# Hybrid decoder step: low weight parts on GpSimd for the last tiles, later splits, longer yields at four places

## Chip, cores and metric

One core of one Trainium2 chip. The metric is device microseconds (us) of one execution, as the median of repeated runs. Engines: PE (TensorE; PEld is its weight load), DVE (VectorE), ACT (ScalarE), POOL (GpSimd), SP (SyncE, which issues most DMAs).

## What is computed

Two layers of a hybrid decoder trunk over 520 tokens (512 of a prompt and 8 samples of one token each), width 2048, float32. Each layer is, cut to what matters:

```python
mod = silu(c) @ w_ada + b_ada                     # shift, scale, gate
h = rms_norm(x, norm_g) * (1 + scale) + shift
proj = h @ w_in                                   # 53 column tiles of 128
att = attend(rope(q), rope(k), v, sinks)          # window 128, 16 query heads, 4 key heads
mixed = cur + (prev - cur) * mu_shift             # r, kr, vr, decay and rate inputs
ys, S_T = wkv_recurrence(r, decay, k_eff, v, kk, a, S0)
y_rw = group_norm(ys) * ln_w + ln_b + bonus
out = concat([att * silu(g_att), y_rw * silu(g_rw)]) @ w_out
x = x + gate * out
```

A final RMSNorm follows; keys, values, recurrent states and shifts are outputs as well.

## The kernel before

The two large products hold weights as the stationary operand, 128x128, and move 260 tokens at a time. To keep float32 precision each weight is split into a high part (rounded) and a low part (the rest), the activations too, and a product is the sum of three: high by high, high by low, low by high. The loop over this is `quarter` (line 372): a weight tile of 2048x128 is done in four quarters of 128x512 weights, and a quarter is 4 x 3 x 2 = 24 matmuls (line 380). A layer has 53 such tiles for `w_in`, in the order of `ORDER`, then 16 for `w_out`. The tiles of a layer come as: the low-rank tile L; then eight groups of three (P: r, kr, v of two recurrent heads) with gate tiles (R, and the first three A) between; then keys and values (K, V, K, V); then eight query tiles (Q); one gate tile A; and the last four A.

**Weights.** `load_w` (line 343) has SP load a quarter's 256 KB into one of four `raw` buffers. `head_w` has ACT cast it to the high part (line 355, four `hi` buffers). `split_w` (line 357) has DVE subtract to get the low part (line 365, three `lo` buffers), and then issues the load that takes the freed `raw` buffer. `quarter` calls `split_w(n + 3)` after its last matmul, so high cast, low part and load stand in their engines' queues right behind the quarter, and the low part has to wait until PE is through with the quarter whose buffer it takes.

**Side work.** Everything else (norms, modulation, attention, the recurrence) is written as Python generators. Each main matmul ticks a counter (`Side.tick`), and at most one generator that is due runs up to its next `yield`, whose value (mostly from the list `W`) is the distance in main matmuls to its next piece. So the order of the work in every engine's queue is fixed by these distances; the engines then run it in order, waiting on each other's results. Some places drain side work, that is emit the rest with no main matmul between: at the gate tile A4 until all eight attentions and all eight chains are done (`RELOAD`), and at the layer's end until the samples are.

The pieces that the change touches:

- `ada` (line 273) computes the modulation. For its last third, run beside the first tiles of a layer, it loads `GA` steps ahead; each step is 40 main matmuls, and the products (line 299) run for two steps together.
- `chain` (line 535), one per pair of recurrent heads: 64x64 triangular inverses are made from two 32x32 inverses each. The matrices go through DRAM (line 647 out by SP, line 662 in by POOL), POOL runs 31 steps of two instructions (lines 670 and 672) on the 32x32 inverses, stores them (line 714), clears `xT` (lines 717, 718) and loads them back (line 721). Then two products join the halves: line 733, a copy on DVE (line 736), `yield W[30]` (4), line 741, a copy (line 745), `yield W[31]` (3). The sequence steps (lines 763 to 787) follow.
- `attend` (line 912), one per query tile: rope, high part of the query on ACT, low parts on DVE (line 931, twice, `yield W[79]` (6) behind each), then scores (lines 949, 950), softmax, transposes (982), products (993).
- `attend_samples` (line 1015), once all query tiles are roped: eight rounds, one per sample: copy of the new key (line 1034), `yield W[61]` (4), scores (1041), softmax, transpose (1060), product (1067). A join of all samples (line 1075) and the gating follow.

In the out projection the first two tiles run quarter by quarter together, and only then does DVE add their residual (line 1190); the third tile takes the first one's accumulator. At the start of layer 0 tiles are done in parts of one quarter, which DVE adds up (line 404).

Of the kernel before, what the change touches and what calls it, by code (L numbers as in the profile page):

```python
# [12 lines left out]
ALU = mybir.AluOpType  # L13
# [6 lines left out]
KT = 16  # L20
# [19 lines left out]
NT = 53  # L40
# [59 lines left out]
ORDER = _order()  # L100
# [4 lines left out]
LOG = 30  # L105
INV = 95
DEPTH = 3
RMS = 29
HQ = 4
LEAD0 = 3  # L110
GA = 1
ADA0 = 70
GROUP = 4
HT = 3
# [17 lines left out]
W = [0, 0, 10, 3, 32, 10, 12, 24, 15, 19, 4, 16, 4, 3, 30, 4, 3, 5, 4, 4, 4, 5, 13, 9, 8, 6, 24, 24, 152, 13, 7, 3, 9, 9, 14, 10, 4, 29, 30, 13, 12, 12, 4, 20, 12, 36, 9, 40, 5, 12, 1, 10, 6, 6, 19, 12, 12, 4, 4, 77, 24, 4, 23, 12, 11, 2, 10, 6, 10, 6, 26, 3, 13, 9, 3, 9, 11, 13, 11, 6]  # L132
# [39 lines left out]
def body(ctx, tc, xt, ct, consts, pars, wada, win, wout, lora, sst, swkv, ck, cv, cvn, fing,  # L172
         o_y, o_kp, o_vp, o_sp, o_sh, o_ks, o_vs, o_vn, o_ss):
    nc = tc.nc
    ve, se, ge, pe, sy = nc.vector, nc.scalar, nc.gpsimd, nc.tensor, nc.sync
# [156 lines left out]
    wseq = []  # L332
# [7 lines left out]
    held = [(NT + KT + i, q) for q in range(HQ) for i in range(2)]  # L340
    raws, his, splits = {}, {}, {}

    def load_w(n):
        if n < len(wseq):
            i, q = wseq[n][:2]
            raws[n] = wp.tile([128, 4, 128], F32, tag="raw", name="raw", bufs=RAWS)
            sy.dma_start(out=raws[n], in_=wsrc[i][:, 4 * q:4 * q + 4, :])
# [9 lines left out]
    def split_w(n):  # L357
        if n < len(wseq):
            hi = his.pop(n)
            head_w(n + 1)  # L360
            if wseq[n] in held:
                lo = t2([128, 512], "wlo", F32R).rearrange("p (k c) -> p k c", k=4)
            else:
                lo = wp.tile([128, 4, 128], F32R, tag="lo", name="lo", bufs=DEPTH)
            ve.tensor_tensor(out=lo, in0=raws.pop(n), in1=hi, op=ALU.subtract)  # L365
            splits[wseq[n]] = (n, hi, lo)
            load_w(n + RAWS)

# [3 lines left out]
    def quarter(ps, key, hh, hl, k0=0, k1=KT, halves=(0, 1)):  # L372


        n, hi, lo = splits[key]
        for k in range(4 * key[1], 4 * key[1] + 4):
            for j, (a, b) in enumerate(((hi, hh[k]), (hi, hl[k]), (lo, hh[k]))):
                for h in halves:
                    stop = k == k1 - 1 and j == 2
                    pe.matmul(ps[:, h, 0:NH], a[:, k % 4], b[:, h * NH:(h + 1) * NH],  # L380
                              start=(k == k0 and j == 0), stop=stop)
                    if not stop:
                        side.tick()
        if key not in held or halves[-1]:
            del splits[key]
        if key not in held or not halves[0]:
            split_w(n + DEPTH)

    def gemm(i, hh, hl, name):

# [108 lines left out]
    def layer(l, hh, hl, xprev, xnext, start, prepare, after):  # L499
# [35 lines left out]
        def chain(p, lw, r, kr, v):  # L535
# [95 lines left out]
            for g in range(2):  # L631
# [8 lines left out]
                for h in range(2):  # L640
                    for a, o in ((atk[g], 64), (atq[g], 0)):
                        ve.tensor_tensor(out=a[:, :, h], in0=pss[h][:, :, o:o + 64],
                                         in1=wmask[:, o:o + 64].unsqueeze(1).to_broadcast([128, 4, 64]),
# [90 lines left out]
            for i in range(2):  # L734
                o = (96, 64)[i]
                ve.tensor_copy(x1[96:128, i], pa[o:o + 32, 0:8])
            yield W[30]
            for e in range(8):
                for i in range(2):
                    o = (64, 96)[i]  # L740
# [2 lines left out]
            for i in range(2):  # L743
                o = (64, 96)[i]
                ve.tensor_copy(flat(xT[i])[64:96, :, 32:64], pa[o:o + 32, 8:16])
            yield W[31]
            y = t2([128, N], "y")
            for c in range(8):
                if c == 6:
# [162 lines left out]
        def attend(P, m, ps):  # L912
# [16 lines left out]
            for u in range(2):  # L929
                us = slice(64 * u, 64 * u + 64)  # L930
                ve.tensor_tensor(out=qq[u][64 - 64 * u:128 - 64 * u], in0=q[us, 0:T], in1=qq[u][us],
                                 op=ALU.subtract)
                yield W[79]
            ya = t2([128, T], "ya")
            col = 8 * P + 2 * m
            kk, kl = kT[P]
            for n0 in range(0, 4, 2):
# [3 lines left out]
                for u in range(2):  # L941
# [3 lines left out]
                    for i in range(2):  # L945
                        n = n0 + i
# [68 lines left out]
        def attend_samples():  # L1015
# [15 lines left out]
            for b in range(B):  # L1031
                load(b + 1)
                for P in range(2):
                    ve.tensor_copy(kc[b][:, P, 128:129], kS[P][:, b:b + 1])
                yield W[61]
                sy.dma_start(out=o_ks[l, :, :, b, :], in_=kc[b][:, :, 1:129])
                ps = ps1("ssc")
                for kv in range(4):
# [455 lines left out]
```

## Time and profile before

| what | value |
|---|---|
| median of 3 runs | 2344.32 us (2335.37 to 2345.83) |
| profiled execution | 2349.78 us, span 2348.0 us |
| mean granted PE clock | 0.975 |
| PE busy | 2223.8 us (95%) |
| PEld busy | 2104.7 us (90%) |
| DVE busy | 1482.8 us (63%) |
| ACT busy | 1057.9 us (45%) |
| POOL busy | 794.7 us (34%) |
| layer 0: w_in tiles, w_out tiles | 45 to 1000.7 us, 1000.8 to 1221.9 us |
| layer 1: w_in tiles, w_out tiles | 1222 to 2141.2 us, 2141.3 to 2330.9 us |

The profile is one execution: the span runs from the first to the last instruction, and the execution is longer by what lies around it. Busy times are shares of the span. A granted clock of 1.00 is 2.4 GHz and 0.50 is 1.2 GHz. In a row of a timeline the bracket is the idle time of the engine before it, and what ended it.

### The profile page before, as it was taken

What the parts mean: (1) busy time and instruction counts of PE and PEld (TensorE: products, weight loads), DVE (VectorE), ACT (ScalarE), POOL (GpSimd) and SP (SyncE); (2) the same over time, 40 slices, a digit from 0 to 9 for tenths busy, and PEclk for the clock granted to TensorE, in tenths of its full rate; (3) what the DMA queues carried; (4) which work ended last, traced back from release to release, by engine and by line L of the source; (5) the groups of instructions that cost most, each with busy time, mean ns of one, the idle gap of its engine ahead of it and who ended that gap; (6) DMA issues with size and microseconds to landing.
All of it is one profiled execution on the core that took longest, in us unless ns stands there. A gap on an engine that the chain in (4) does not pass through costs nothing. (4 is left out here: it accounts for less than half of the span.)

```text
span 2348.0 us, 53897 instructions
## 1 busy us (share of the span) xinstructions
PE 2223.8 (95%) x20708; PEld 2104.7 (90%) x20708; DVE 1482.8 (63%) x3712; ACT 1057.9 (45%) x2346; POOL 794.7 (34%) x1428
## 2 busy tenths in 40 slices
PE   5999999999999999999999999999999999999997
PEld 4899989999989898889989989889999999899997
DVE  3464677767785886533365456577776778765346
ACT  3244354554455555422244435345555446553222
POOL 2105655766566000000011526655776440000112
PEclk8999999999999999999999999999999999999998
DMA  9945555323333225777762455543332322244335
GB/s 363 348 149 169 166 158 160 104 89 97 102 95 95 64 79 158 225 225 245 244 211 77 129 156 163 165 138 106 94 96 88 96 90 77 60 131 138 113 115 180
DMA packets 229329, 337.92 MB, mean 144 GB/s; under 512 B 59696, under 2 KB 80304, under 8 KB 228912
## 3 DMA queue, kind: packets, MB, share of 16 engines
q1 hardware_dynamic: 223184, 321.89, 44.1%
q0 software_dynamic: 5888, 12.59, 1.8%
q8 instruction: 163, 2.67, 0.5%
q14 instruction: 94, 0.77, 0.1%
HBM read 303.90 MB, written 32.56 MB: 143 GB/s over the span
## 5 line engine op out<-in xcount | busy, mean ns | idle before, releaser
L365 DVE TENSOR_TENSOR lo<-raw,hi 128x512 fp32r<-128x512 f32 x568 | 414.5, 730 | 454.0 <-PE psO L380 135.4
L355 ACT CAST hi<-raw 128x512 fp32r<-128x512 f32 x568 | 350.8, 619 | 632.2 <-PE psP L380 211.2
L380 PE MATMUL psP<-hh,lo 128*128 128x260 f32 x1408 | 307.7, 292 | 0.0
L380 PE MATMUL psP<-hl,hi 128*128 128x260 f32 x1408 | 305.0, 292 | 0.0
L380 PE MATMUL psP<-hh,hi 128*128 128x260 f32 x1408 | 304.1, 292 | 0.2 <-ACT dm L518 0.2
L672 POOL TENSOR_TENSOR xi<-xi,tmp 128x248 f32<-128x248 f32 (+30 forms) x496 | 280.8, 566 | 38.9
L670 POOL TENSOR_TENSOR tmp<-f,xi 128x248 f32<-128x248 f32 (+30 forms) x496 | 258.7, 521 | 86.6 <-DMA f<-d 49.1
L380 PEld LDWEIGHTS psP<-hh,lo 128*128 128x128 f32 x1408 | 225.7, 192 | 6.3 <-issue 3.7
L380 PEld LDWEIGHTS psP<-hl,hi 128*128 128x128 f32 x1408 | 225.1, 192 | 5.9 <-issue 3.3
L380 PE MATMUL psO<-yh,hi 128*128 128x260 f32 x1024 | 225.1, 286 | 3.6 <-DVE xsn L1193 3.6
L380 PEld LDWEIGHTS psP<-hh,hi 128*128 128x128 f32 x1408 | 224.6, 192 | 3.1 <-issue 1.2
L380 PE MATMUL psO<-yh,lo 128*128 128x260 f32 x1024 | 225.2, 286 | 1.7 <-DVE lo L365 1.7
L380 PE MATMUL psO<-yl,hi 128*128 128x260 f32 x1024 | 224.5, 285 | 0.0
L380 PEld LDWEIGHTS psO<-yh,hi 128*128 128x128 f32 x1024 | 166.6, 191 | 5.7 <-issue 5.6
L380 PEld LDWEIGHTS psO<-yh,lo 128*128 128x128 f32 x1024 | 166.7, 191 | 3.6 <-DVE lo L365 1.9
L380 PEld LDWEIGHTS psO<-yl,hi 128*128 128x128 f32 x1024 | 166.6, 191 | 1.6 <-issue 1.6
L1329 POOL TENSOR_SCALAR yo<-xnew,fg 128x260 f32<-128x260 f32 x32 | 31.2, 978 | 391.6 <-DVE xnew L1190 377.4
L445 POOL TENSOR_TENSOR rmsr<-rmsv,mhalf 128x3 f32<-128x3 f32 x6 | 5.6, 938 | 464.4 <-DMA raw<-in_wout_dram 449.3
L787 ACT COPY y<-seq 64x64 f32<-64x64 f32 x256 | 52.6, 205 | 195.5 <-DVE mbd L781 136.1
L299 PE MATMUL adps<-rawa,cT 128*32 128x128 f32 (+1 forms) x2048 | 112.5, 348 | 23.5 <-DMA rawa<-in_wada_dram 23.0
L380 PE MATMUL psQ<-hl,hi 128*128 128x260 f32 x512 | 117.6, 295 | 0.0
L380 PE MATMUL psQ<-hh,lo 128*128 128x260 f32 x512 | 114.3, 294 | 0.0
(362 smaller groups left out, 5463.6 us busy)
## 6 DMA issues: line engine op xcount, KB each, us to landing
raw<-in_win_dram SPq DMA_DIRECT2D x424, 256.0 KB, 3.3
rawa<-in_wada_dram SPq DMA_DIRECT2D x384, 256.0 KB, 4.8
raw<-in_wout_dram SPq DMA_DIRECT2D x152, 256.0 KB, 3.6
f<-d POOLq DMA_DIRECT2D x64, 128.0 KB, 3.6
gd<-th SPq DMA_DIRECT2D x22, 260.0 KB, 2.5
gr<-gd SPq DMA_DIRECT2D x22, 260.0 KB, 3.5
x<-in_xt_dram SPq DMA_DIRECT2D x16, 260.0 KB, 5.3
yd<-rk SPq DMA_DIRECT2D x16, 260.0 KB, 3.4
```

The source lines that it names most:

```text
L299: pe.matmul(ap[32 * g:32 * g + 32, 0:w], cT[:, kk, :], raw[g * w // 512][:, c:c + w], start=(kk == 0), stop=(kk == KT - 1))
L355: se.copy(out=his[n], in_=raws[n])
L365: ve.tensor_tensor(out=lo, in0=raws.pop(n), in1=hi, op=ALU.subtract)
L380: pe.matmul(ps[:, h, 0:NH], a[:, k % 4], b[:, h * NH:(h + 1) * NH], start=(k == k0 and j == 0), stop=stop)
L445: ge.tensor_tensor(out=r[:, 0:3], in0=v[:, 0:3], in1=mhalf[:, 0:3], op=ALU.pow)
L670: ge.tensor_tensor(out=tv, in0=f[:, s:s + 1, s + 1:32].to_broadcast([128, 8, 31 - s]), in1=xi[:, :, s:s + 1].to_broadcast([128, 8, 31 - s] ...
L672: ge.tensor_tensor(out=xi[:, :, s + 1:32], in0=xi[:, :, s + 1:32], in1=tv, op=ALU.add)
L787: se.copy(out=y[hs, 64 * c:64 * c + 64], in_=yp[hs, h])
L1329: ge.tensor_scalar(out=out[h][m // 2][:, m % 2], in0=xn[:, h * NH:h * NH + NH], scalar1=fg[:, m:m + 1], scalar2=None, op0=ALU.mult)
```

## The change

The low part of a quarter is subtracted on GpSimd instead of DVE when its tile lies from the first query tile to the last gate tile of a layer (13 tiles, 52 quarters, in each layer). `split_w` is no longer called at a quarter's end but behind the ninth matmul of the next one. The modulation loads two steps ahead instead of one. Four distances grow: `W[30]` 4 to 8, `W[31]` 3 to 12, the second `W[79]` 6 to 18, `W[61]` 4 to 12.

```diff
--- before.py
+++ after.py
@@ -105,10 +105,13 @@
 LOG = 30
 INV = 95
 DEPTH = 3
+
+FREE = (ORDER.index(("Q", 0, 0)), len(ORDER))
+LATE = 9
 RMS = 29
 HQ = 4
 LEAD0 = 3
-GA = 1
+GA = 2
 ADA0 = 70
 GROUP = 4
 HT = 3
@@ -340,6 +343,8 @@
     held = [(NT + KT + i, q) for q in range(HQ) for i in range(2)]
     raws, his, splits = {}, {}, {}
 
+    due = []
+
     def load_w(n):
         if n < len(wseq):
             i, q = wseq[n][:2]
@@ -362,7 +367,9 @@
                 lo = t2([128, 512], "wlo", F32R).rearrange("p (k c) -> p k c", k=4)
             else:
                 lo = wp.tile([128, 4, 128], F32R, tag="lo", name="lo", bufs=DEPTH)
-            ve.tensor_tensor(out=lo, in0=raws.pop(n), in1=hi, op=ALU.subtract)
+            t = wseq[n][0] % (NT + KT)
+            eng = ge if FREE[0] <= t < FREE[1] else ve
+            eng.tensor_tensor(out=lo, in0=raws.pop(n), in1=hi, op=ALU.subtract)
             splits[wseq[n]] = (n, hi, lo)
             load_w(n + RAWS)
 
@@ -373,6 +380,7 @@
 
 
         n, hi, lo = splits[key]
+        done = 0
         for k in range(4 * key[1], 4 * key[1] + 4):
             for j, (a, b) in enumerate(((hi, hh[k]), (hi, hl[k]), (lo, hh[k]))):
                 for h in halves:
@@ -381,10 +389,13 @@
                               start=(k == k0 and j == 0), stop=stop)
                     if not stop:
                         side.tick()
+                    done += 1
+                    if done == LATE and due:
+                        split_w(due.pop())
         if key not in held or halves[-1]:
             del splits[key]
         if key not in held or not halves[0]:
-            split_w(n + DEPTH)
+            due.append(n + DEPTH)
 
     def gemm(i, hh, hl, name):
 
@@ -734,7 +745,7 @@
             for i in range(2):
                 o = (96, 64)[i]
                 ve.tensor_copy(x1[96:128, i], pa[o:o + 32, 0:8])
-            yield W[30]
+            yield 2 * W[30]
             for e in range(8):
                 for i in range(2):
                     o = (64, 96)[i]
@@ -743,7 +754,7 @@
             for i in range(2):
                 o = (64, 96)[i]
                 ve.tensor_copy(flat(xT[i])[64:96, :, 32:64], pa[o:o + 32, 8:16])
-            yield W[31]
+            yield 4 * W[31]
             y = t2([128, N], "y")
             for c in range(8):
                 if c == 6:
@@ -930,7 +941,7 @@
                 us = slice(64 * u, 64 * u + 64)
                 ve.tensor_tensor(out=qq[u][64 - 64 * u:128 - 64 * u], in0=q[us, 0:T], in1=qq[u][us],
                                  op=ALU.subtract)
-                yield W[79]
+                yield W[79] * (1 + 2 * u)
             ya = t2([128, T], "ya")
             col = 8 * P + 2 * m
             kk, kl = kT[P]
@@ -1032,7 +1043,7 @@
                 load(b + 1)
                 for P in range(2):
                     ve.tensor_copy(kc[b][:, P, 128:129], kS[P][:, b:b + 1])
-                yield W[61]
+                yield 3 * W[61]
                 sy.dma_start(out=o_ks[l, :, :, b, :], in_=kc[b][:, :, 1:129])
                 ps = ps1("ssc")
                 for kv in range(4):
```

## Rows read from the trace of the kernel before

**Rows 1.** Windows 742:1000.7 and 1895.8:2141.2, their sum: busy us by engine.

```profile
sum 504.10, PE 478.73 PEld 446.83 DVE 366.08 ACT 269.48 POOL 17.31; mean PE 239.36 PEld 223.42 DVE 183.04 ACT 134.74 POOL 8.65
```

**Rows 2.** Waits, whole run: waiter <- releaser: us, times, longest us.

```profile
PE t2a L741 <- DVE x L736: 14.6, 9, 2.2
PE seq L774 <- DVE sv L772: 12.9, 12, 2.0
PE sc L949 <- DVE qq L931: 5.6, 7, 2.0
PE psS L380 <- DVE part L404: 3.6, 2, 1.8
PE psO L380 <- DVE xsn L1193: 3.6, 2, 1.8
PE ssc L1041 <- DMA ktc<-in_ck_dram: 1.8, 1, 1.8
PE ssc L1041 <- DVE ktc L1034: 1.5, 1, 1.5
```

**Rows 3.** Timeline of DVE at a join: start us, us, instruction, xcount.

```profile
1707.79 0.68 DVE L365 TENSOR_TENSOR lo<-raw,hi 128x512 fp32r<-128x512 f32 x1
1708.51 0.87 DVE L736 COPY x<-t2a 32x256 f32<-32x256 f32 x2
```

**Rows 4.** Timeline of PE around the same join.

```profile
1707.41 0.40 PE L380 MATMUL psP<-hl,hi 128*128 128x260 f32 x2
1709.43 0.69 PE L741 MATMUL t2a<-xT,x 32*32 32x32 f32 x32 [1.61 <-DVE x L736]
1712.07 0.64 PE L380 MATMUL psP<-hl,hi 128*128 128x260 f32 x2
```

**Rows 5.** Windows: PE, PEld, DVE, ACT, POOL busy us; granted clock; DMA share, GB/s.

```profile
485.10:491.90 6.80, 6.80 (x34) 6.80 (x33) 1.95 (x9) 2.59 (x5) 3.67 (x6) 0.50 0.33 114
1710.40:1713.90 3.50, 3.50 (x20) 3.50 (x18) 1.59 (x5) 1.10 (x3) 0.86 (x2) 0.51 0.63 190
```

**Rows 6.** Chain that ended last: gate matmuls behind the samples join.

```profile
2136.96 4.47 PE psA L380 x37
```

**Rows 7.** Timeline of DVE behind two out-projection tiles.

```profile
2164.60 0.69 DVE L365 TENSOR_TENSOR lo<-raw,hi 128x512 fp32r<-128x512 f32 x1 [2.20 <-PE psO L380]
2165.21 0.87 DVE L1190 SCALAR_TENSOR_TENSOR xnew<-psO,mod,xo 128x260 f32<-128x260 f32 x2
```

**Rows 8.** Waits of PE, 160 to 2340 us: modulation weights.

```profile
PE adps L299 <- DMA rawa<-in_wada_dram: 3.4, 3, 1.7
```

**Rows 9.** DVE low parts by line: 742 to 1000 us, then 168.3 to 742.

```profile
L365 DVE TENSOR_TENSOR lo<-raw,hi 128x512 fp32r<-128x512 f32 x52 | 35.9, 691 | 27.5 <-PE psA L380 17.4 <-ACT ptb L985 3.7 <-ACT y L842 1.9
L365 DVE TENSOR_TENSOR lo<-raw,hi 128x512 fp32r<-128x512 f32 x132 | 100.7, 763 | 59.2 <-PE psP L380 27.6 <-issue 10.0 <-PE psR L380 7.4
```

**Rows 10.** Window of the chains' stretch: columns as in rows 5.

```profile
168.30:742.00 573.70, 553.98 (x5241) 528.68 (x5240) 397.62 (x915) 285.24 (x595) 351.22 (x647) 0.98 0.42 124
```

**Rows 11.** Groups by line, POOL, a product of that shape: busy us, mean ns.

```profile
L474 POOL TENSOR_TENSOR xn<-x,rstd 128x512 f32<-128x512 f32 x4 | 5.2, 1291 | 46.3 <-PE adps L299 46.3
```

**Rows 12.** Timeline of POOL: last step of the last chain's inversion, both layers.

```profile
745.71 0.22 POOL L672 TENSOR_TENSOR xi<-xi,tmp 128x8 f32<-128x8 f32 x1
1900.41 0.22 POOL L672 TENSOR_TENSOR xi<-xi,tmp 128x8 f32<-128x8 f32 x1
```

**Rows 13.** Timeline of PE: first matmul with a query low part, both layers.

```profile
742.74 0.39 PE L380 MATMUL psQ<-hh,lo 128*128 128x260 f32 x2
1896.31 0.40 PE L380 MATMUL psQ<-hh,lo 128*128 128x260 f32 x2
```

**Rows 14.** Timeline of SP's queue: a weight load, then the second matrix transfer.

```profile
697.70 0.35 SPq L347 DMA_DIRECT2D raw<-in_win_dram  x1
698.10 0.92 SPq L647 DMA_DIRECT2D d<-atk  x2
```

**Rows 15.** Timeline of DVE: the last copy that this transfer carries.

```profile
695.48 0.41 DVE L642 TENSOR_TENSOR atk<-atp,cst 128x256 f32<-128x256 f32 x1
```

## The prediction

> **What bounds the kernel now.** I read the time by stage first, then the list of PE's waits, then timelines around the longest waits, then the granted clock behind them. In the two stretches of query and attention-gate tiles [rows 1] PE is busy 479 of 504 us while DVE is busy 366 and POOL 17: the bound is PE's stream of matmuls, and whatever can be won is time in which PE stands still, or runs at half clock. The list of PE's waits [rows 2] puts names to it: the joining product at L741 waits 14.6 us for a copy on DVE, the sequence step at L774 12.9, the scores at L949 5.6, the out projection 3.6 for the residual, the partial tiles 3.6, the sample scores 3.3. In the timeline of one join [rows 3, 4] DVE does a low part (L365, 0.68 us) just ahead of the copy that PE waits for; PE waits 1.61 us, and afterwards pairs of matmuls take 0.64 us instead of 0.40. That is the clock: it was granted at 0.50 (1.2 GHz) in that stretch and in the longer one at 485 [rows 5]. Between 100 and 2300 us there are twenty such stretches, fifteen of 3.4 us and five of 6.8, each behind a wait of PE of 1.3 us or more; a stretch costs half its length, so 1.7 or 3.4 us on top of the wait. They cost some 43 us together.
>
> **The change part by part.** A plain matmul takes 0.121 us (37 in 4.47 us [rows 6]); I call that a step of the side schedule.
>
> *Splits nine matmuls later.* No work changes; DVE's, ACT's and SP's queues are re-ordered. Where two tiles of the out projection end together, the low part waits 2.20 us for PE's last matmul and the residual (L1190), ready earlier, stands behind it [rows 7]; behind it again PE waits, 1.79 us, twice [rows 2]. With the low part nine matmuls later the residual runs during PE's last quarter: 3.6 us gone, and two stretches of 3.4 us (3.4 us): **-7** (bounds 3.6 and 7). The partial tiles (3.6 us, two waits) lose only the low part's 0.6 each: 1.2, and up to 3.4 of clock; I take **-3**. Six of the nine waits at L741 have a low part in front as in rows 3: -3.6, below. At the sequence steps the low part leaves the front of some copies and comes nearer to others, and the longer yields shift the chain by 13 steps against the tiles: bounds -8 and +8 of 18.6 us, taken as **0**.
>
> *Joining products.* Twice W[30] puts four more steps, 0.48 us, between L733 and L741: nine waits, **-4.4**, with the low parts **-3.6**. Seven of these waits were followed by half clock (three stretches of 6.8 us, four of 3.4: 34 us, a cost of 17). Waits of 1.5 to 2.2 us become 0.4 to 1.4; I take half of the cost back, **-9** (bounds 0 and 17). Four times W[31] meets no wait in the list; its cover is the chain's slack, nothing.
>
> *Scores and samples.* 18 steps instead of 6 after the second query low part are 1.45 us more; the longest wait is 2.0: **-5** of 5.6. Twelve instead of four before the sample scores are 1.0 us: of 3.3 us (two waits) **-2**, and one half-clock stretch, **-1**.
>
> *Modulation loads one further ahead.* PE's waits for these weights inside the layers sum to 3.4 us [rows 8], one followed by half clock: 2.3 and 1.7, **-4**. One more pair of loads is in flight; nothing waits for SP there.
>
> *Low parts on GpSimd.* 52 per layer leave DVE, at 691 ns each where POOL is idle [rows 9]; the other row there, 763 ns, is from a stretch in which POOL is busy 351 of 574 us [rows 10]: 72 us off DVE. What PE waits for on DVE in those stretches and is not priced above is small: **-2**. On GpSimd the nearest row is a product of the same shape, 1.29 us [rows 11]; POOL is nearly empty there [rows 1], and a quarter takes PE over 3 us, so steadily it is hidden. The exception is the start. The last chain's inversion is 62 instructions on POOL and ends at 745.9 and 1900.6 us [rows 12], while PE needs the first query low part at 742.74 and 1896.31 [rows 13]. Counting the yields, all steps of the inversion are emitted before that low part, so it queues behind them. But the inversion itself starts earlier: the second transfer of its matrices is emitted six matmuls behind a quarter's end, behind a weight load that waits for the low part [rows 14], though its data are there at 695.9 [rows 15]; with the load nine matmuls behind, it goes 2 us sooner, and I take that for both layers. So the low part is done at 745.9 - 2 + 1.3 = 745.2 and at 1899.9: PE waits 2.5 and 3.6 us. To this come 1.7 us of half clock each, and what I won between the chain's start and there is lost, since GpSimd now sets that moment: 2.5 us each. **+14.5** (bounds 0, if the inversion is done in time, and 24, without the earlier transfer and with the longer stretch).
>
> *What comes late next.* The scores' extra 12 steps make the last attention miss the gate tile that drains for it, by one product: **+2** (1 us per layer for a copy between transpose and product). The samples' eight rounds grow by 64 steps, and their last join stands only 37 matmuls ahead of the gates' end [rows 6]: half a round now runs with no matmul beside it, a transpose, a copy, a product and a join, about 2.5 us of latency per layer plus 1.7 of clock, less what these waits cost today: **+5** (bounds 0 and 12).
>
> **Sum:** -7 -3 -8 -9 -5 -3 -4 -2 = -41, +14.5 +2 +5 = +21.5: about -19.5. The profiled execution took 2349.8 us (span 2348.0), 5.5 above the median 2344.3 of the runs shown; I take the sum from the median: **2325 us**.
>
> **Rivals.** *The clock does not come back.* The waits shorten but stay long enough for the half-clock stretches, or re-form at the sequence steps. Then 16.9 us of the gains fall away (3.4, 1.8, 9, 1 and 1.7 of clock): -2.6 is left, 2342 us. For it: joins wait for different DVE work in each chain. Against: the waits in front of these stretches are the longest on the list, and they are those that shrink.
>
> *GpSimd takes the lock.* By [rows 9, 10] DVE and POOL do hinder each other, mildly: 763 ns against 691. If every GpSimd low part held DVE for its 1.29 us, 134 us would replace the 72 taken off, DVE would be busy 428 of 504 us, and the waits on DVE there (the scores' 5.6, two of the joins, the sample copy's 1.5, some 10 us) would double instead of falling: 20 us more than the sum, 2345 us. The Trainium skill speaks for this (SBUF — State Buffer, section on the two separate sides): the port pair of VectorE and GpSimd is an exclusive lock, held for a whole instruction, against VectorE operations with two SBUF inputs. By that rule, the trace agrees in direction (763 against 691 ns); but many DVE operations in those stretches read PSUM or one SBUF tensor.
>
> *The head of the queries (slower).* The same queue as above, without the earlier transfer. Behind the inversion stand the store, four memsets, a wait for the store to land and four DMA issues, all in POOL's order among the tile's low parts. If three of the first four quarters wait (5, 5 and 4 us), each with 3.4 us of half clock, that is 24 us per layer, 48, with the 5 lost upstream and the 7 of the late ends 60 against 41: +19, 2363 us. It decides the sign from 15 us per layer on. For it: 62 instructions that are emitted faster than POOL does them. Against: the later low parts have a quarter of 3.5 us each to catch up.
>
> **How the numbers follow.** Forecast 0.50 (2308 to 2333); clock stays 0.25; lock 0.08; head 0.12; better than all of it, with every stretch back at full clock and the head free, 0.05, under 2306. The range that holds 8 in 10 goes from 2306 to 2347: it takes in both middle rivals and leaves out most of the slower one. About 0.5%, 11.7 us, is what a measurement of this kernel can tell from no change: faster than 2332.6 has the forecast, the best case and a little of the first rival, 0.57; slower than 2356 the head, 0.12; the rest, 0.31, between.
>
> **What would show it.** Right: no wait of PE for the residual behind the paired tiles; L741's waits under 6 us in all; the scores' nearly gone; fewer than twelve half-clock stretches; 104 low parts on POOL at 1.3 to 1.6 us; one wait of PE of 2 to 4 us at each first query tile, for a POOL low part. Wrong: a POOL wait of over 8 us there; PE waits at the samples' last join over 5 us; as many half-clock stretches as now; or DVE's mean for two-input work in those stretches up by a third.

## The result: 0.5% slower, and the profile after

| | before | after |
|---|---|---|
| median of 20 runs each, us | 2341.7 (2333.4 to 2348.1) | 2352.1 (2343.5 to 2360.0) |
| ratio, 95% interval | | 1.0052 (1.0041 to 1.0063) |
| profiled execution, its span, us | 2349.8, 2348.0 | 2348.0, 2346.2 |
| mean granted clock, profiled | 0.975 | 0.985 |
| busy us: PE, DVE, POOL | 2223.8, 1482.8, 794.7 | 2209.8, 1480.3, 935.0 |

The forecast was 2325 (2306 to 2347): the change came out slower than the whole range. The two profiled executions hide it, being equal to 2 us. The one of before lay above all 20 runs of the table: its mean clock was 0.975, where 29 further runs of that kernel had a median of 0.980. At two levels of clock, 0.005 of 2348 us is up to 12 us lost to half clock that a usual run does not lose. So the comparison of the two traces flatters the change by some 8 to 12 us, and the sizes below come from timed runs.

The traces still say where to look. Between 100 and 2300 us the half-clock stretches fell from twenty to nine, and all stages outside the queries and gates became shorter by some 35 us together. The query and gate stretches became longer. First, the windows of these two stretches after (columns: PE, PEld, DVE, ACT, POOL busy; clock; DMA share, GB/s); they answer to [rows 1].

```profile
729.80:998.40 268.60, 247.75 (x2231) 228.31 (x2229) 182.13 (x527) 134.36 (x368) 75.10 (x69) 0.98 0.43 131
1872.40:2141.00 268.60, 240.75 (x2101) 224.50 (x2099) 179.45 (x526) 134.47 (x368) 78.96 (x77) 0.98 0.32 94
sum 537.20, PE 488.50 PEld 452.81 DVE 361.58 ACT 268.83 POOL 154.06; mean PE 244.25 PEld 226.41 DVE 180.79 ACT 134.41 POOL 77.03
```

They last 537.2 us against 504.1. 104 low parts of 0.691 us, 72 us, have left DVE; its busy time fell by 4.5. Something else on DVE grew. The groups of DVE by line and shape in layer 0's stretch (busy us, mean ns) name it, first before, then after:

```profile
L954 DVE CUSTOM_DVE_ANT_0 s<-sc,cst,par 128x256 f32<-128x256 f32 x48 | 21.9, 481 | 4.4 <-PE sc L950 4.2
L931 DVE TENSOR_TENSOR qq<-q,qq 64x512 fp32r<-64x512 f32 x16 | 11.0, 686 | 0.5
L973 DVE TENSOR_SCALAR s<-s,es 128x128 f32<-128x128 f32 x16 | 3.9, 283 | 0.3
L958 DVE TENSOR_SCALAR mx<-mx 128x4 f32<-128x4 f32 x16 | 2.7, 169 | 0.5
L918 DVE COPY qs<-q 128x8 f32<-128x8 f32 x8 | 1.4, 176 | 0.3
```

```profile
L965 DVE CUSTOM_DVE_ANT_0 s<-sc,cst,par 128x256 f32<-128x256 f32 x48 | 21.8, 480 | 8.2 <-PE sc L961 8.1
L942 DVE TENSOR_TENSOR qq<-q,qq 64x512 fp32r<-64x512 f32 x16 | 16.1, 1004 | 6.8 <-ACT qq L938 6.5
L984 DVE TENSOR_SCALAR s<-s,es 128x128 f32<-128x128 f32 x16 | 10.0, 665 | 0.3
L969 DVE TENSOR_SCALAR mx<-mx 128x4 f32<-128x4 f32 x16 | 5.5, 342 | 0.4
L929 DVE COPY qs<-q 128x8 f32<-128x8 f32 x8 | 4.2, 527 | 0.3
```

The operation that reads PSUM (s from sc) kept its 480 ns. The others shown, with all operands in SBUF and two inputs or one, grew by half to three times, down to a copy of 8 columns. Not every operation of that kind grew: q from q and qa, two inputs of 128x520, took 701 ns before and 700 after, since it began ahead of the low parts that it met, as in the second moment below. Three moments of the changed kernel show how: the timelines of POOL, of DVE and, for the last moment, of PE (start us, duration us), one fence for each engine.

```profile
812.95 1.28 POOL L372 TENSOR_TENSOR lo<-raw,hi 128x512 fp32r<-128x512 f32 x1 [4.33 <-PE psQ L388]
...
822.87 1.82 POOL L372 TENSOR_TENSOR lo<-raw,hi 128x512 fp32r<-128x512 f32 x1 [4.49 <-PE psQ L388]
...
1913.91 1.29 POOL L372 TENSOR_TENSOR lo<-raw,hi 128x512 fp32r<-128x512 f32 x1 [4.12 <-ACT hi L360]
```

```profile
813.05 1.20 DVE L969 TENSOR_SCALAR mx<-mx 128x4 f32<-128x4 f32 x1
...
822.86 0.70 DVE L881 TENSOR_TENSOR q<-q,qa 128x520 f32<-128x520 f32 x1
...
1914.00 1.75 DVE L824 TENSOR_TENSOR st<-st,sa 128x512 f32<-128x512 f32 x1
...
1916.06 1.01 DVE L984 TENSOR_SCALAR s<-s,es 128x128 f32<-128x128 f32 x4
```

```profile
1916.41 0.52 PE L993 MATMUL pT<-cst,s 128*128 128x128 f32 x2 [1.50 <-DVE s L984]
```

At 1913.91 a low part begins on POOL and ends at 1915.20; DVE's state update begins 0.09 later and takes 1.75 us instead of 0.69: it ends 0.55 behind POOL. Behind it in DVE's queue stand the sum, the reciprocal and s, and PE waits 1.50 us for s. At 813.05 a product of four columns, 0.17 us elsewhere, ends 0.02 behind POOL's 814.23. At 822.87 it is the other way round: DVE began first, and POOL's low part takes 1.82 us and ends 1.13 behind DVE's end. Of the DVE instructions that began with 0.3 us or more of a low part still to run, all 17 of s, all 9 copies qs and all 8 of qq ended at a fixed distance behind POOL's end (0.08 to 0.15, 0.03 and 0.55 us). None of 17 that read PSUM for s, and none of 11 copies of a single column, did. This is a hold for one whole instruction, not a slowdown. It is what the Trainium skill says (SBUF — State Buffer, section on the two separate sides), and the trace agrees: one port pair of the two engines, given to whichever starts first, the other blocks fully.

PE's waits after, 100 to 2340 us, answer to [rows 2] (PE's L744 is L733 of before, L752 is L741, L774, L781 and L785 are L763, L770 and L774):

```profile
PE seq L781 <- DVE rr L775: 15.3, 13, 2.2
PE pT L993 <- DVE s L984: 11.4, 16, 1.6
PE psQ L388 <- POOL lo L372: 7.5, 2, 5.6
PE t2a L744 <- DVE x L738: 6.3, 5, 1.7
PE pnb L1086 <- DVE z L1082: 3.3, 2, 2.1
PE t2a L752 <- DVE x L747: 2.8, 3, 1.1
PE seq L785 <- DVE sv L783: 1.3, 3, 0.7
```

The joins' 14.6 at L741 and the sequence step's 12.9 are nearly gone (2.8 and 1.3; the first product has 6.3, 5.1 before), but the sequence step between them, 1.2 us on the list of before, now waits 15.3. The transposes' wait for s went from 2.7 to 11.4 (4.1 once the low parts are back on DVE, below). POOL's queue holds PE at the head of the queries, 1.9 us in layer 0 and 5.6 in layer 1. There, on POOL and then on PE:

```profile
1872.53 0.55 POOL L681 TENSOR_TENSOR tmp<-f,xi 128x56 f32<-128x56 f32 x1
...
1877.11 0.22 POOL L683 TENSOR_TENSOR xi<-xi,tmp 128x8 f32<-128x8 f32 x1
1877.28 1.26 POOL L372 TENSOR_TENSOR lo<-raw,hi 128x512 fp32r<-128x512 f32 x1
```

```profile
1878.60 0.80 PE L388 MATMUL psQ<-hh,lo 128*128 128x260 f32 x2 [5.58 <-POOL lo L372]
```

Behind the wait the clock falls to half: windows at the first time of [rows 5], now at full clock, and at this place.

```profile
485.10:491.90 6.80, 6.80 (x58) 6.70 (x58) 5.93 (x12) 2.83 (x7) 6.17 (x9) 1.00 0.22 68
...
1877.80:1884.60 6.80, 6.00 (x28) 6.01 (x29) 0.56 (x2) 1.61 (x4) 6.53 (x11) 0.50 0.49 156
```

### The profile page after: what moved, and what is told of

It reads as the page before. It is cut to its first block, busy times and chain, and to the rows that moved or that the text cites. A ratio compares the mean times of both kernels' runs of the same rounds, so it can differ in the third digit from the quotient of the medians.

```text
span 2346.2 us, 53881 instructions
## 1 busy us (share of the span) xinstructions
PE 2209.8 (94%) x20708; PEld 2087.7 (89%) x20708; DVE 1480.3 (63%) x3608; ACT 1049.0 (45%) x2346; POOL 935.0 (40%) x1532
## 5 line engine op out<-in xcount | busy, mean ns | idle before, releaser
L372 DVE TENSOR_TENSOR lo<-raw,hi 128x512 fp32r<-128x512 f32 x464 | 343.5, 741 | 216.6 <-PE psO L388 106.2
L388 PE MATMUL psP<-hh,lo 128*128 128x260 f32 x1408 | 302.1, 289 | 0.0
L372 POOL TENSOR_TENSOR lo<-raw,hi 128x512 fp32r<-128x512 f32 x104 | 138.8, 1335 | 355.9 <-PE psQ L388 141.4
L302 PE MATMUL adps<-rawa,cT 128*32 128x128 f32 (+1 forms) x2048 | 106.7, 341 | 19.5 <-DMA rawa<-in_wada_dram 19.4
L792 DVE SCALAR_TENSOR_TENSOR mbd<-mbd,pend,seq 64x64 f32<-64x64 f32 x224 | 62.7, 280 | 95.3 <-PE seq L788 92.5
```

The source lines that it names most:

```text
L302: pe.matmul(ap[32 * g:32 * g + 32, 0:w], cT[:, kk, :], raw[g * w // 512][:, c:c + w], start=(kk == 0), stop=(kk == KT - 1))
L372: eng.tensor_tensor(out=lo, in0=raws.pop(n), in1=hi, op=ALU.subtract)
L792: ve.scalar_tensor_tensor(out=m1[hs, hs], in0=m0[hs, hs], scalar=pend8[hs, c:c + 1], in1=mn[hs, hs], op0=ALU.mult, op1=ALU.add)
```

## The experiments

The theory was that GpSimd's low parts lengthen DVE's own work and so PE's waits; the rivals, that only the head of the queries costs, or that the later splits or the longer distances do. All times are medians; "us of before" are 2341 times the ratio to the kernel before on the same chip, less 2341. In these units the change is +12.2 (9.6 to 14.7).

**GpSimd's part.** All low parts back on DVE, the rest of the change kept:

```diff
-FREE = (ORDER.index(("Q", 0, 0)), len(ORDER))
+FREE = (len(ORDER), len(ORDER))
```

> All low parts are back on DVE; late splits, the second modulation step ahead and the four longer distances stay. Theory (POOL's low parts lengthen DVE's own work and so PE's waits): the query and gate stretches took 504 us before and 537 after in the two profiles, all else gained some 35; without POOL's low parts the stretches come back to about 500, so about 2317 us, 25 to 35 under the changed kernel, and DVE's 128x128 normalising (s, 642 ns after) is back near 284 ns. Rival (only the head of the queries): the two waits of 7.5 us and their half clock go, 11 us, about 2341 us. Rival (distances too long at the gates' end): 7 us stay in layer 1's gates, 2324 us or more.

Measured: 2333.0, ratio 0.9972 (0.9955 to 0.9989), -6.6 us. GpSimd's low parts so cost 18.8 us, where the theory had 25 to 35, and s is back at 284 ns. And the rest of the change brings 7 us, where the theory's 2317 would have been 24: a second surprise. Layer 1's last four gate tiles, to the first matmul of the out projection, still take 89 us against 81 before. The second rival put that down to the longer distances; the traces of later runs without the two late ones have 87 with late splits and 84 without (87 with the distances), so these hold 3 of the 8 us.

From the second query tile on only:

```diff
-FREE = (ORDER.index(("Q", 0, 0)), len(ORDER))
+FREE = (ORDER.index(("Q", 0, 1)), len(ORDER))
```

> GpSimd's low parts begin one tile later, at the second query tile, when the last inversion is long done. Rival (head of the queries): both waits of PE for POOL at the first query tile (1.9 and 5.6 us) go and with them the loss, so the same time as with all low parts on DVE, within 4 us. Theory (DVE lengthened by POOL): only these 7.5 us and up to 4 of half clock go; 48 of 52 low parts still stand beside DVE's work: about 2342 us, some 20 to 25 above the kernel with all low parts on DVE; s stays above 500 ns.

Measured: 2342.8, 1.0001 (0.9985 to 1.0018), +0.2. The head of the queries is 12.0 of the 18.8 us (with what the first tile's low parts hold), and no wait for POOL's lo is left among PE's. 6.8 us remain, so neither theory nor rival alone is enough; the theory named 20 to 25 for this.

GpSimd's low parts as the only edit on the kernel before:

```diff
+FREE = (ORDER.index(("Q", 0, 0)), len(ORDER))
...
-            ve.tensor_tensor(out=lo, in0=raws.pop(n), in1=hi, op=ALU.subtract)
+            t = wseq[n][0] % (NT + KT)
+            eng = ge if FREE[0] <= t < FREE[1] else ve
+            eng.tensor_tensor(out=lo, in0=raws.pop(n), in1=hi, op=ALU.subtract)
```

> The kernel before with the 104 low parts on GpSimd as the only edit; splits stay at the quarter's end. Theory: slower than before by the loss of the two stretches without the gains elsewhere: 25 to 40 us, about 2375 us, s near 640 ns. Rival (late splits are what costs in the query stretch, POOL is harmless): within 12 us of before, which is the head's two waits.

Measured: 2381.0, 1.0170 (1.0149 to 1.0191), +39.8. Alone it costs twice what it costs in the change: with the splits at the quarter's end and short distances, the scores wait 14.2 us for DVE's qq (5.6 before), a wait that the change does not have. That is a part of the difference; the rest was not traced.

The same low part in four short instructions on GpSimd:

```diff
+            raw = raws.pop(n)
+            if eng is ge:
+                for k in range(4):
+                    ge.tensor_tensor(out=lo[:, k], in0=raw[:, k], in1=hi[:, k], op=ALU.subtract)
...
```

> The changed kernel, but each low part on GpSimd is done as four instructions of 128x128 instead of one of 128x512: same data, same engine, same time in the queue or a little more. Theory A (a DVE instruction is held for as long as GpSimd's instruction of that moment lasts): the holds become a quarter as long, s (642 ns) falls below 420 ns, the longest s from 1369 to under 700, and about half of the 19 us between the changed kernel and the one with all low parts on DVE come back: about 2342 us. Rival B (the two engines share a rate, so the amount of data counts): s stays within 50 ns of 642 and the time within 4 us of 2352. Rival C (four instructions cost GpSimd more): low parts arrive late, PE waits for POOL beyond the two first query tiles, slower than 2356.

Measured: 2342.5, 1.0023 (1.0006 to 1.0041), +5.4: 6.8 of the 18.8 come back. POOL and DVE in layer 0's stretch, against 1322 ns for one instruction, 665 for s and 342 for mx after the change:

```profile
L375 POOL TENSOR_TENSOR lo<-raw,hi 128x128 fp32r<-128x128 f32 x208 | 101.5, 519 | 140.9 <-PE psQ L393 49.9 <-PE psA L393 35.3 <-ACT hi L360 27.0
L989 DVE TENSOR_SCALAR s<-s,es 128x128 f32<-128x128 f32 x16 | 5.7, 401 | 0.3
L974 DVE TENSOR_SCALAR mx<-mx 128x4 f32<-128x4 f32 x16 | 3.8, 236 | 0.4
```

GpSimd works longer on the same data, 1.95 us a low part (101.5 over 52), and DVE is hindered less: rival B falls, the length of a single GpSimd instruction is what counts. (One shape is the exception: over both layers s of 128x256, 349 ns alone, went from 418 to 467.) PE still waits 6.2 us for POOL's low parts at the head.

A subtraction on GpSimd that no engine waits for, with all low parts on DVE (`dum` stands for a bfloat16 tile that the code makes there):

```diff
+            if eng is ge:
+                ge.tensor_tensor(out=dum, in0=cst[:, 0:512], in1=cst[:, 512:1024], op=ALU.subtract)
+            ve.tensor_tensor(out=lo, in0=raws.pop(n), in1=hi, op=ALU.subtract)
```

> All low parts on DVE, and in place of each GpSimd low part GpSimd subtracts two constant 128x512 tensors into a buffer that nobody reads. Nobody waits for GpSimd. Theory (contention of the two engines for SBUF): about as bad as the changed kernel without its two waits at the head: 2343 to 2350 us, s above 550 ns, while DVE's reads of PSUM keep their length within a tenth. Rival (the loss comes from waiting for GpSimd's results): as with all low parts on DVE, 2333 within 4, s near 290 ns.

Measured: 2381.8, 1.0192 (1.0167 to 1.0217), +44.9. Much worse than any theory had it, and not the clean measurement that was meant: nothing holds the dummies back, so from 747 us forty-five ran in one train of 68 us, and as many in layer 1, and the last chain's own POOL work queued between them (PE waited 5.4 us for that). Gated like the real low part, from the second query tile on:

```diff
-                ge.tensor_tensor(out=dum, in0=cst[:, 0:512], in1=cst[:, 512:1024], op=ALU.subtract)
+                ge.tensor_tensor(out=dum, in0=cst[:, 0:512], in1=hi, op=ALU.subtract)
```

> All low parts on DVE; from the second query tile on GpSimd subtracts, for each quarter, the high part from a constant, into a buffer that nobody reads: it waits for ACT's cast as the real low part does, so it does not run in trains, and no engine waits for its result. Theory (holds alone): the run with all low parts on DVE plus what the start at the second query tile left, 10 us, and DVE has the low parts too: 2341 to 2350 us, s above 500 ns. Rival (loss comes from waiting for results): 2333 within 4.

Measured: 2368.1, 1.0114 (1.0093 to 1.0136), +26.7, 33 above the run with low parts on DVE. Nobody waits for these results (PE's list puts 0.9 us down to them), so the loss is the holds, with the half clock behind the waits that they cause. It is larger than expected, since DVE's low parts are now there to be held: eleven that began with 0.3 us or more of a dummy still to run took 1.26 us each, s is at 600 ns in layer 0's stretch, DVE is busy 416.7 us in the two stretches against 367.5. Both known costs taken out of the changed kernel (four instructions, and the start at the second query tile):

> The changed kernel with each GpSimd low part in four instructions and the first query tile's low parts on DVE: both known costs removed, GpSimd still does 96 low parts. Theory (head and long holds are all of it): the run with low parts on DVE, 2333 us, within 4, and 2 to 6 us above it if short holds still cost a little; s below 420 ns. Rival (a third cost, such as low parts that arrive late all along): 2341 us or more, with waits of PE for POOL's lo.

Measured: 2334.9, 0.9977 (0.9962 to 0.9991), -5.4: 17.6 of the 18.8 us are back, with 96 low parts still on GpSimd. Within the intervals, head and long holds are all of it. PE's standing time in the two stretches (length less PE busy) says the same: 48.7 us after, 33.6 with low parts on DVE, and here 33.0:

```profile
sum 518.30, PE 485.28 PEld 451.10 DVE 336.61 ACT 268.84 POOL 207.63; mean PE 242.64 PEld 225.55 DVE 168.30 ACT 134.42 POOL 103.82
```

The holds have not gone: DVE's work other than low parts, summed over the two stretches, is 342 us before, 399 after and 370 here. What is gone is the wait behind them: the transposes wait 4.1 us for s, as with all low parts on DVE, and 11.4 after.

**The rest of the change.** Single parts on the kernel before, and combinations; all with the low parts on DVE. Late splits alone, on the kernel before:

```diff
+                    if done == LATE and due:
+                        split_w(due.pop())
...
-            split_w(n + DEPTH)
+            due.append(n + DEPTH)
```

> Late splits as the only edit on the kernel before. The prediction priced them at 7 for the residual, 3 for the partial tiles, 3.6 for low parts ahead of joins, and 2 us from the earlier transfer that here meets no use: 14 us with some clock, so about 2328 us. Rival (late splits only re-order DVE's queue, what leaves one wait enters another): within 6 us of before. Rival (late splits starve PE of low parts or of weights): slower than before, with waits of PE for lo or hi above 5 us.

Measured: 2340.3, 0.9994 (0.9978 to 1.0011), -1.4. The waits move:

```profile
PE seq L785 <- DVE sv L783: 16.3, 13, 1.9
PE t2a L752 <- DVE x L747: 13.7, 11, 1.9
PE sc L960 <- DVE qq L942: 8.6, 12, 2.0
PE ssc L1052 <- DMA ktc<-in_ck_dram: 6.4, 2, 4.2
PE psO L388 <- DVE lo L372: 5.1, 5, 1.7
```

The residual's 3.6 us are gone, as forecast, and the same accumulator matmuls now wait 5.1 for the low part (1.7 before); the joins keep their wait, the scores and sample scores wait 3.0 and 3.1 more (the latter 3.3 before), and the partial tiles' 3.6 became 2.5.

The four distances and `GA`, without these lines:

> Low parts on DVE and splits back at the quarter's end: the distances and the second modulation step ahead alone. The prediction has 4.4 and 9 for the joins (part of it through the late splits), 5 for scores, 3 for samples, 4 for modulation, against 7 for the late ends: about -17, so 2324 us. Theory from the run with late splits alone (1 us): with or without them it is the same, 2333 to 2336 us. Rival (late splits are what makes the longer distances work, by the low part ahead of a join): 2339 us or more.

Measured: 2340.8, 0.9998 (0.9980 to 1.0015). No gain. Then two of the four distances back, so that `W[30]`, `W[31]` and `GA` are left:

```diff
-                yield W[79] * (1 + 2 * u)
+                yield W[79]
...
-                yield 3 * W[61]
+                yield W[61]
```

> As the run before it, with the distances behind the query's low parts and ahead of the sample scores back at 6 and 4: only the joining products' distances and the second modulation step ahead are left. By the prediction 5 and 3 are lost and 7 of late ends won back: within 2 us of the run before it. Theory (late ends cost more than they were priced at, 7 us in layer 1's gates alone): 4 to 8 us faster than the run before it, about 2328 us. Rival (the scores' wait was worth its 5 us, the late ends cost nothing): 5 to 8 us slower.

Measured: 2328.1, 0.9953 (0.9935 to 0.9972), -11.0: the two later distances cost 10.5 us. The theory's 2328 us was met, with more than its 4 to 8 us of gain; the prediction's 1 us was not. `GA` taken away as well, so the joins alone:

```diff
-GA = 2
+GA = 1
```

> The two joining distances as the only edit on the kernel before. The prediction has 4.4 us of wait and up to 9 of clock for them and 4 for modulation: 4 us slower than joins and modulation together, 2332 us. Rival (the waits re-form at the next step of the sequence, as the trace of that run has 13.5 us there, so the joins are worth nothing and modulation all): 2337 us or more. Rival (modulation worth nothing): within 2 of 2328.

Measured: 2322.3, 0.9930 (0.9911 to 0.9950), -16.4: the lowest median of all and below every expectation, though its interval overlaps that of joins with `GA`. And that line alone, the other way round, on the kernel before:

```diff
-GA = 1
+GA = 2
```

> Two modulation steps loaded ahead instead of one, as the only edit on the kernel before. The prediction: 4 us faster, 2337 us, and no wait of PE for modulation weights inside the layers. Theory from joins alone against joins with modulation: 5 us slower, 2346 us. Rival (the difference of those two was chance): within 3 us of before.

Measured: 2340.6, 1.0006 (0.9989 to 1.0023): nothing, although PE's wait for modulation weights (3.4 us before) is gone from its list, as forecast; the wait at L733 went from 5.1 to 7.9. The 5 us between the two runs above were inside their intervals. The two joining distances one by one, each on the kernel before:

```diff
-            yield W[30]
+            yield 2 * W[30]
```

> Only the distance ahead of the second joining product doubled (4 to 8), on the kernel before. The prediction: 4.4 us of wait and 9 of clock, about 2328 us, and waits at that product from 14.6 to under 8 us. Rival (the second distance is what helps): within 4 us of before, 2341.

```diff
-            yield W[31]
+            yield 4 * W[31]
```

> Only the distance behind the last joining product four times as long (3 to 12), on the kernel before. The prediction: nothing, 2341 us. Rival (it gives the copy behind the last product, and the sequence step that reads it, time, and moves the sequence waits of 12.9 us): 8 us or more faster, 2333 or less.

Measured: 2332.5, 0.9971 (0.9953 to 0.9990), -6.8; and 2341.6, 0.9995 (0.9978 to 1.0012). Of the two, the first is the one that helps, as the prediction had it; together they do more than the sum, by about the width of the intervals. PE's waits with the first alone, with the second alone, and with both (in the last fence L713, L742 and L779 are L704, L733 and L770):

```profile
PE seq L774 <- DVE sv L772: 14.9, 14, 1.8
PE t2a L733 <- DVE x L727: 9.7, 10, 1.4
```

```profile
PE seq L770 <- DVE rr L764: 12.3, 10, 1.7
PE t2a L741 <- DVE x L736: 1.6, 3, 1.1
```

```profile
PE seq L779 <- DVE rr L773: 13.6, 13, 2.1
PE t2a L742 <- DVE x L736: 6.5, 6, 1.7
PE av L713 <- ACT sv L706: 5.7, 6, 1.7
PE seq L779 <- DVE rr L776: 3.7, 5, 1.4
```

The wait at L741, 14.6 before, is down to 1.3, 1.6 and 1.1 in the three: also with the second distance alone, which leaves that of L741 as it was and wins no time. DVE at one join before, and then with the second distance alone, shows why:

```profile
555.19 0.69 DVE L813 TENSOR_TENSOR st<-st,sa 128x512 f32<-128x512 f32 x1
555.92 0.87 DVE L736 COPY x<-t2a 32x256 f32<-32x256 f32 x2
```

```profile
552.64 0.87 DVE L736 COPY x<-t2a 32x256 f32<-32x256 f32 x2
553.54 0.69 DVE L810 TENSOR_TENSOR st<-st,vz 128x512 f32<-128x512 f32 x1
```

In all nine joins that waited before, one to three of the state updates of another pair's chain (L810, L811, L813, 0.69 us each, 20 in all) ran between L733's products and the copy; the low parts (six, 0.68 us) are the smaller piece. With the second distance alone none of these updates runs there at any of the 16 joins, with the first alone at 2 of them, and with both at 5, where the wait is 0.7 us or less. With late splits alone they run there at ten of the eleven joins that wait over 0.3 us, and the wait stays. So both distances cure L741 by moving two chains against each other. With the first alone, L774 keeps its wait and L733 has 9.7 instead of 5.1; with both, L774 is at 1.9 but L770 at 17.3 in two groups, and av, a product ahead of the joins that waits nowhere before, has 5.7. Over joins and sequence steps the lists go from 39.5 us to 35.1 (first) and 32.3 (both); with av the latter is 38.0. So the chain waits hardly less. What changed most is the clock: with both, the half-clock stretches between 100 and 2300 us sum to 24 us in that trace, 85 in that of before, and the timed runs have a median clock of 0.987 against 0.980; 0.007 of 2341 is up to 16 us.

Combinations, by the same lines: joins and late splits; these and `GA = 2`; these and `W[79] * (1 + 2 * u)`; and, instead of that, `3 * W[61]`:

> The joining distances and the late splits, nothing else. If late splits are worth what they are alone (1 us): 2320 to 2323 us, no different from the joins alone (2322). The prediction's price (7 for the residual, 3 for the partial tiles, 3.6 at the joins): 2310 us. Rival (late splits move the chain's products against the tiles and bring waits back at the sequence steps): 2325 us or more.

> Both distances back, late splits kept: joins, modulation and late splits. If costs add up: 2333 less the 12.6 us that the two distances cost without late splits, about 2320 us, and 8 us under joins and modulation without late splits (2328). Rival (late splits alone were worth 1 us): 2326 to 2330 us. Rival (what one part wins another takes, since waits move along the queue): between 2330 and 2335.

> Low parts on DVE, late splits, joins, modulation and the scores' distance stay as in the changed kernel; only the distance ahead of the sample scores is back at 4. Without it the last join of the samples stands 64 steps earlier. Theory (the samples' late end is the cost): 6 to 9 us under the run with all distances (2333), about 2325 us, the wait at the join of all samples (3.3) under 1.5 us. Rival (the scores' distance is the cost): within 3 us of 2333. The prediction had 5 of late end against 3 of waits won: 2 us faster.

> The other half: the distance behind the second query low part is back at 6, that ahead of the sample scores stays 12. Theory (samples' late end is the cost): 2330 to 2336 us; scores wait again, 3 to 9 us. Rival (the scores' distance, which pushes the last attention past the gate tile that drains for it, is the cost): about 2325 us. The prediction had 5 won at the scores against 2 of late drain: 3 us slower, 2336 us.

Measured: 2328.3, 0.9948 (0.9930 to 0.9966); 2326.8, 0.9938 (0.9917 to 0.9958); 2329.0, 0.9955 (0.9939 to 0.9970); 2336.7, 0.9987 (0.9973 to 1.0001). Late splits are worth little anywhere: +4.2 us on the joins, -3.5 on joins with `GA`, -6.1 with all distances, all about as wide as the intervals. Taking both late distances out of the run with all (-6.6) wins 7.9 us; taking out `W[61]` alone wins 3.9, taking out `W[79]` alone loses 3.6, each within the intervals. Of the expectations, the first run met its rival (2325 or more), the second the rival that prices late splits at 1 us, the third lies between its theory and its rival, and the fourth met the prediction's 2336.

What `W[61]` costs at the layer's end stands in the traces. In every run with it at 12 the last of the samples' work comes behind the last gate matmul, and the out projection begins 2.7 to 3.2 us after that matmul in each layer (4.4 and 5.9 us with `W[79]` back); in every run with it at 4 the out projection follows at once. PE in layer 1 of the run with all low parts on DVE:

```profile
2120.55 0.41 PE L388 MATMUL psA<-hh,lo 128*128 128x260 f32 x2
...
2123.48 0.41 PE L1086 MATMUL pnb<-z,cst 128*128 128x64 f32 x2 [1.27 <-DVE z L1082]
2123.70 0.48 PE L388 MATMUL psO<-yh,hi 128*128 128x260 f32 x2
```

## Why the prediction was wrong

By its own terms, in us of before:

| step | forecast | measured |
|---|---|---|
| GpSimd: relief on DVE | -2 | +6.8 (holds) |
| GpSimd: head of the queries | +14.5 | +12.0 |
| joining products, wait and clock | -8 and -9 | -16.4 (without late splits) |
| late splits (residual, partial tiles) | -7 and -3 | -1.4 alone; +4.2, -3.5, -6.1 in pairs |
| scores, samples, less late ends | -8 and +7 | +7.9 and +10.5 in two pairs |
| modulation | -4 | +1.4 |

Joins alone, `GA` alone, late splits alone, the late distances (9) and GpSimd (18.8) sum to +11.4; the change was +12.2. So the parts nearly add up, each of them good to some 4 to 6 us. Against the forecast of -19.5 the miss is 31.7 us, and by the rows the largest pieces are the late distances (10), GpSimd's holds (9), the late splits (9) and the modulation (5), less 2 for head and joins together: the lock is less than a third, and the rest are gains that were counted and did not come.

**The head** had the right mechanism and nearly the right sum, in part by luck: PE waited 1.9 and 5.6 us where 2.5 and 3.6 were forecast. Layer 1 missed the earlier transfer, as its inversion stood to the tiles as before (at 56 columns 0.5 us before PE came). These 7.5 us and the half clock behind them (stretches of 3.4 and 6.8 us, a cost of 5.1) make 12.6 against 12.0 measured, which leaves nothing for the 5 us "lost upstream". The bound of 24 does not follow from its terms, which add up to 21.9.

**"What PE waits for on DVE is small: -2"** failed. The mechanism stood among the rivals, as the lock with a chance of 0.08, and its own sign came true for qq (up by 35% over both layers, from 686 to 929 ns; all two-input work of 512 or 520 columns on DVE other than low parts went from 691 to 851). It was put aside because "many DVE operations in those stretches read PSUM or one SBUF tensor". PSUM readers are free; operations with one SBUF input are not: s, mx and qs are held. The Trainium skill has that too (the same page, section on who interferes with whom): it names copies and tensor-scalar operations among those that can enter a two-port mode, and so contend for the shared pair, when their operands meet that mode's conditions. The rival's price of 20 us over the sum was wrong as well, in size (9) and in place: the scores did not wait, the transposes behind s did. And the means of [rows 9], 691 and 763, made it look mild. The trace of before had the answer in single instructions, DVE's low part and POOL's product at one moment:

```profile
468.03 1.39 DVE L365 TENSOR_TENSOR lo<-raw,hi 128x512 fp32r<-128x512 f32 x1
```

```profile
467.84 1.03 POOL L659 TENSOR_TENSOR kb<-kb,pend 128x512 f32<-128x512 f32 x1
```

Held to POOL's end at 468.87 and 0.55 more; all 18 low parts of before that began inside such a product ended 0.55 us behind it. The mean is mild only because such products are rare, and most steps of the inversion are short: the 116 low parts that began inside one took 0.68 to 1.14 us.

**"Residual gone, -7"**: the wait went, as forecast, and the time did not: the low part that had stood ahead of it became late instead. The step that failed is that nothing was named as late next. The partial tiles lost 1.1 us of wait, as forecast; the scores and sample scores took 6.1 more. The sequence steps, "taken as 0" between bounds of -8 and +8, came out near that, with 21.4 us of wait against 19.8.

**Scores and samples, -8**: this failed, in the gain. The wait for qq went (3.7 and 2.4 us in the two runs without the late distances), but ACT's ycs stands in its place at the scores (2.9 and 2.0), and the sample scores still wait for the loads of ktc. All waits at the scores and in the sample rounds, the last join included, rise with the two distances, from 13.8 to 16.3 us with late splits and from 9.5 to 11.8 without. The samples' late end, "about 2.5 us of latency per layer", was sized right: 2.7 to 3.2. The rest of the 7.9 and 10.5 us stays open.

**Modulation, -4**: the wait went, the time did not; other waits re-formed.

**The joins** came out at the forecast size and not by the forecast way, so a part of that is luck. The 8 us of wait held 3.6 from the late splits, which the run of 16.4 does not have. L741's wait went, but the step "four more steps, 0.48 us" for each of nine waits and 3.6 for the low parts missed what stood in front of the copy: the state updates of another chain, which each distance moves out of the way, also the one that was counted as nothing. The waits re-formed at L770, L733 and av, and the clock came back all the same; why both distances win more than each is not shown.

**The clock** came back in part: nine stretches, "fewer than twelve" as forecast. But the forecast's gain was read from one execution whose clock was below a usual run's: timed runs after have 0.984 against 0.980, up to 9 us of the 16.9 that were counted, where the two traces have 0.985 against 0.975. So the rival "clock does not come back" was half right, and right in that the waits re-formed at the sequence steps.

## What to carry to other kernels

Before moving work from DVE to GpSimd, look in the trace for DVE instructions of SBUF operands that start while a long GpSimd instruction runs: if they end at a fixed distance behind its end, the move can cost DVE the rest of each GpSimd instruction that it meets (here 57 us of DVE's time, for 72 freed), and what it costs the kernel depends on who waits behind the held instruction. If the work must go there, cut it into short instructions, and do not start it while another long GpSimd job is queued. A wait that is cured in an in-order schedule can stand at the next step, as with the residual, the joins and the modulation here; measure each edit alone, and count clock gains over many runs, not from one trace.

## What the hardware showed that was not expected

The hold works both ways and to the instruction: POOL's low part ended 1.13 to 1.15 us behind the DVE instruction that it met, for 14 of the 14 that took over 1.38 us, and DVE's two-input instructions of 512 columns 0.55 behind POOL's. It reaches a copy of 8 columns and a product of 4, but not copies of one column (none of 11), reciprocals (none of 3), or anything that reads PSUM. Cut in four, the same low part takes 1.95 us of GpSimd instead of 1.32, and costs the kernel 6.8 us less.
